# Values as a seven-product group: both groups opened on two token blocks, two convolution tiles moved into the heads

## The chip, the cores and the metric

The kernel runs on one core of a Trainium2 chip. The metric is device time in microseconds, from the median of several executions. One execution was profiled; its span runs from the first to the last instruction.

## The reference

One decoder layer over 512 tokens and 1024 channels, batch 1, all in float32. Cut to what matters here:

```python
u = _rmsnorm(h, norm1_g[l])
proj = u @ w_in[l]
a_glu, q, k, v, r, g_low, gate_a, gate_b = _split_cols(proj)
c = a_glu[..., :CONV_CH] * jax.nn.sigmoid(a_glu[..., CONV_CH:])
c = _causal_dwconv(c, conv_dw_w[l], conv_dw_b[l])            # width 31
c = jax.nn.silu(_layernorm(c, conv_ln_g[l], conv_ln_b[l]))
y_conv = c @ w_conv_out[l]
gk = jax.nn.log_sigmoid(g_low @ w_gate_up[l] + b_gate[l]) / GATE_NORMALIZER
o = _gla_chunked(qh, kh, vh, gkh)                            # 4 heads, chunks of 64
o = o * lax.rsqrt(jnp.mean(o * o, -1, keepdims=True) + EPS) * gla_norm_g[l]
o = o.reshape(bsz, seq, GLA_VDIM) * jax.nn.silu(r)
y_gla = o @ w_gla_out[l]
merged = jax.nn.sigmoid(gate_a) * y_conv + jax.nn.sigmoid(gate_b) * y_gla
h = h + merged @ w_o[l]
# then a channel mixer (up-projection, convolution of width 3, gate, down-projection) and a last RMSNorm
```

The change is in how `a_glu` (16 column tiles of 128), `v` and `r` (1024 columns each) are computed from `u`.

## The kernel before

**Arithmetic.** TensorE multiplies float32 operands rounded to a reduced format. Each operand is split into a high part (rounded by ACT) and a low part (the rest, subtracted by DVE), and `mm3` (lines 363 to 365) issues three matmuls: low by high, high by low, high by high. A weight block is 512 KB (128 partitions by 1024). `load` starts its transfer on SP's queue into one of four `raw` tiles, `split_weight` splits it into `whi` and `wlo` (four tiles each), and `weight` hands out the next block of one long list, `order`, having split those ahead of it. For blocks in `ADDED` the low part is not subtracted by DVE: ACT writes the negated raw block and POOL's queue adds the original onto its rounded form by an accumulating DMA.

**Tiles.** Convolution, query, key and gate projections are column tiles (`col_tile`): 128 output channels by 512 tokens, 24 matmuls for one weight block. Values and out-gate are laid out with tokens on partitions, because the heads read them so.

**Seven block products.** For names in `SEVEN` a product of two 2 by 2 block matrices is done with seven block products instead of eight (steps a11, a12, s1, n2, s4, n3, a22). The sums of activation blocks (`form`, `place`) are made by DVE, the sums of weight blocks by accumulating DMAs on POOL's queue (`sum_on`, `add_n3`) into the tile that `kept` names. Before, the out-gate `w_r` is such a group (`unit`), with blocks read from a relaid copy (`rows_r`) that 16 transfers from memory to memory on SP's queue (`lay_rows`) write early in the kernel.

**Order.** In the opening the order on PE, ACT, DVE and SP is written out by hand (`manual_schedule`): RMSNorm of four blocks of 128 tokens, their transposition, and the values' first 512 columns for all four token blocks (`v_block`, matmuls of line 624; the first two token blocks unnormalized, with the scale applied when the bank is read). Outside it a scheduler orders each engine. After the opening come the eight convolution tiles (gate and value block each), the low-rank decay projection, the out-gate's seven products with the gate arithmetic between them (`gate`, `GATE_AT`), then four heads. Between the heads' stages (`between`) stand matmuls that don't depend on them: the values' last 512 columns (`late_values`) and four gate tiles.

**Filling DVE.** The depthwise convolution is 30 DVE passes of 0.73 us per channel tile (line 740). These, the activation sums and the layer norm are `chains` of small jobs; every `weight` call lets `fill` emit as many as `RATES` says for that name, behind the latest instruction in `pace`.

Of the kernel before, what the change touches and what calls it, by code (L numbers as in the profile page):

```python
# [17 lines left out]
P = 128  # L18
# [19 lines left out]
RATES = {"w_glu": 6.2, "w_r": 0.3, "w_low": 0.0, "w_v": 5.0, "w_qk": 4.2, "w_gb": 6.0, "w_gla": 6.5, "w_ga": 9.0}  # L38
# [5 lines left out]
ADDED = {("w_glu", 2 * k) for k in range(1, KT)} | {(name, m) for name in ("w_gb", "w_gla") for m in range(KT)}  # L44
# [3 lines left out]
SEVEN = {"w_o": KT // 2, "w_down": FT // 2, "w_r": KT // 2}  # L48
# [5 lines left out]
R_STEPS = [("a11", 0), ("a11", 1), ("a12", 0), ("s1", 0), ("s1", 1), ("a12", 1)] + LATE  # L54
# [4 lines left out]
GATE_AT = [("a11", 1), ("a12", 0), ("n2", 1)]  # L59
# [16 lines left out]
def trunk_layer(ctx: ExitStack, tc: tile.TileContext, a: dict, out: bass.AP):  # L76
# [88 lines left out]
    order = [("w_v", j) for j in range(KT // 2)]  # L165
    order += [("w_glu", 2 * k + j) for k in range(KT) for j in (1, 0)]
    order += [("w_low", 0), ("w_low", 1)]
    order += [("w_r", (O_PAIRS, step, d)) for step, d in R_STEPS]
    for h in range(HEADS):
        late_v = [("w_v", KT // 2 + 2 * h + j) for j in range(2)]  # L170
        late_b = [("w_gb", 2 * (h - 2) + j) for j in range(2)]
        q, k = ("w_qk", 2 * h), ("w_qk", 2 * h + 1)
        order += [q, late_v[0], k, late_v[1]] if h == 0 else [q, k] + (late_v if h == 1 else late_b)
# [14 lines left out]
    def load():  # L188
        if len(raws) < len(order):
# [8 lines left out]
            if j is not None:  # L198
                raw = raw_tile()
                nc.sync.dma_start(raw, a[name][j])  # L200
# [17 lines left out]

    LOADS = {"a11": (0, 0), "a12": (1, 0), "n2": (1, 1), "n3": (0, 1)}

    def load_block(name, pairs, step, d):

        if step not in LOADS:
            return None
        src = block(name, pairs, d, *LOADS[step])
        n = src.shape[-1]
        if step == "a11":
            dst = keep_tile(name)[:, :n]
            kept[pairs, d] = dst
        else:  # L230
            dst = raw_tile()[:, :n]
        nc.sync.dma_start(dst, src)
        if step == "n3":
            kept[pairs, d, "n3"] = dst
            if name != "w_r":
                add_n3(name, pairs, d)
        if step == "n2":
            kept[pairs, d, "b22"] = dst
        return dst

    def add_n3(name, pairs, d):
        nc.gpsimd.dma_start(kept[pairs, d, "n3"], block(name, pairs, d, 1, 1), accum_op=ALU.add)

    def operand(name, raw, pairs, step, d):

        if step == "s4":
            return kept[pairs, d, "b22"]
        if step == "n2" and name != "w_r":
            nc.vector.tensor_tensor(kept[pairs, d], kept[pairs, d], raw, ALU.add)
        return raw if step in ("a12", "n3") else kept[pairs, d]  # L250
# [15 lines left out]
    def sum_on(name, pairs, step, d):  # L266

        where = {"a11": (0, 1), "n2": (1, 0)}
        if name == "w_r":
# [3 lines left out]
        if step in where:  # L273
            nxt = block(name, pairs, d, *where[step])
            nc.gpsimd.dma_start(kept[pairs, d], nxt, accum_op=ALU.add)

    def split_weight(between=None):
        if len(ready) < len(order):
# [34 lines left out]
            if order[len(ready)] in ADDED:  # L313
                nc.scalar.activation(lo, raw, AF.Copy, scale=-1.0)  # L314
# [15 lines left out]
    def weight(name, j, ahead=LOOK):  # L330
# [4 lines left out]
        fill(RATES.get(name, RATE))  # L335
# [4 lines left out]
    room = [0.0, 0]  # L340
    after = []

    def fill(n):
        room[0] += n
        while chains and room[0] > 0:
# [6 lines left out]
            if not chain:  # L352
                chains.remove(chain)
                if not chains and after:
# [147 lines left out]
    def turn_gain(i, bank):  # L502
        nc.tensor.transpose(bank[:, :KT], rows8[:KT, i * P : (i + 1) * P], ident[:KT, :KT])
        nc.vector.tensor_copy(gains[:, i * KT : (i + 1) * KT], bank[:, :KT])

    raise_clock(WARM)
    accs = [mm_bank() for _ in range(NT)]
    turn_gain(0, accs[2])
# [5 lines left out]
    def rms(t):  # L514
        ss = small(2, "ss")
        for j in range(2):
            nc.scalar.activation(junk(T), xs[t][j], AF.Square, scale=1.0 / 32.0, accum_out=ss[:, j : j + 1])
        v = small(1, "var")
        nc.vector.scalar_tensor_tensor(v, ss[:, 0:1], EPS, ss[:, 1:2], ALU.add, ALU.add)
        return rsqrt(v, 1)  # L520

    plain, r1 = {}, {}
# [55 lines left out]

    def renormed(t):
        rb = ax_bank()[:, :P]  # L580
        nc.tensor.matmul(rb, r1[t].to_broadcast([P, P]), ident, start=True, stop=True)
        rb = rb.unsqueeze(1).to_broadcast([P, 4, P])
        for g in range(2):
            nc.vector.tensor_tensor(into_whole(t, g)[0], by_token(unscaled[t, g]), rb, ALU.mult)
        for g in range(2):
            f, parts = into_whole(t, g)
            split_by(f, *parts)

    def gained_normed(t):
        for g in range(2):  # L590
            gain = gains[:, g * 4 : g * 4 + 4].unsqueeze(2).to_broadcast([P, 4, P])
            nc.vector.tensor_tensor(into_whole(t, g)[0], by_token(banks[t][g]), gain, ALU.mult)
        for g in range(2):
# [20 lines left out]
    def v_block(j, *ts, parts=None, more=False):  # L614
        for t in ts:
            src = as_landed(t) if t < 2 else tokens(t)
            ks = (2 * j, 2 * j + 1)
            todo = [(k, p) for p in parts for k in ks] if parts else [(k, p) for k in ks for p in ALL]
            for n, (k, p) in enumerate(todo):
                product(t, j, k, src, *p, j == 0 and n == 0 and not more, j == KT // 2 - 1 and n == len(todo) - 1)  # L620

    def product(t, j, k, src, a_low, w_low, first, last):
        w = ws[j][w_low][:, (k % 2) * T : (k % 2 + 1) * T]
        nc.tensor.matmul(accs[t], src(k)[a_low], w, start=first, stop=last)  # L624
# [1008 lines left out]
```

## Time and profile before

| | |
|---|---|
| median of three runs | 831.43 us (831.42 to 832.16) |
| the profiled execution's own time | 831.21 us |
| its span | 829.5 us, 10901 instructions |
| matmul records on PE | 4066 |
| mean granted TensorE clock | 0.997 |
| data moved | 127.21 MB, mean 153 GB/s |

PE is the matmul stream, PEld its weight loads, DVE, ACT and POOL the other engines, SP the engine that issues most transfers. A matmul's record spans its passage through the array and overlaps the next one's, so the distance of starts tells more than the duration. A row of a timeline or a chain gives start, duration and what ran; `x24` merges that many instructions; what stands in brackets is the idle time before it and what ended it.

### The profile page before, as it was taken

How to read it: one execution, taken by the hardware profiler on the slowest of the kernel's cores; microseconds unless marked ns; L12 is line 12 of the kernel's file. 1: busy time of each engine (PE TensorE's matmuls, PEld its weight loads, DVE VectorE, ACT ScalarE, POOL GpSimd, SP SyncE). 2: the span in 40 equal slices, each digit the busy share in tenths (PEclk: the TensorE clock that was granted, in tenths of full speed). 3: DMA queues.
4: the chain of work that ended last, by engine and by line, in shares of the span. 5: the costliest groups of instructions: out<-in, count | busy, mean ns of one | idle time of the engine just before them, and what ended most of it. 6: DMA issues, size and time to landing. Idle time of an engine off the chain costs nothing.

```text
span 829.5 us, 10901 instructions
## 1 busy us (share of the span) xinstructions
PE 818.6 (99%) x4066; PEld 692.3 (83%) x4066; DVE 667.5 (80%) x988; ACT 450.8 (54%) x648; POOL 106.2 (13%) x127
## 2 busy tenths in 40 slices
PE   9999999999999999999999999999999999999996
PEld 7888887888888888888888898888788888988885
DVE  6999966989899991875789788679858788588896
ACT  6843337762533553148544668655456543667554
POOL 2000102000111121000001012111112011220011
PEclk9999999999999999999999999999999999999998
DMA  9975547723546578221447639256825646657562
GB/s 340 303 205 143 137 110 170 210 101 101 128 110 153 133 195 199 102 82 54 143 97 189 189 119 262 68 145 153 216 87 148 171 87 219 153 153 196 136 126 102
DMA packets 43973, 127.21 MB, mean 153 GB/s; under 512 B 4272, under 2 KB 12736, under 8 KB 43920
## 3 DMA queue, kind: packets, MB, share of 16 engines
q1 hardware_dynamic: 33232, 88.82, 30.4%
q0 software_dynamic: 10512, 37.49, 25.5%
q8 instruction: 32, 0.52, 0.2%
q14 instruction: 21, 0.17, 0.1%
q10 hardware_dynamic: 176, 0.20, 0.1%
HBM read 124.40 MB, written 6.29 MB: 158 GB/s over the span
## 4 chain that ended last, share of the span: by engine, by line
PE 85%; DVE 5%; issue 4%; DMA 3%; ACT 2%; POOL 1%; POOLq 0%; SPq 0%; ACTq 0%; DVEq 0%
PE mm L363 24%; PE mm L364 24%; PE mm L365 24%; PE mm L624 3%; PE ax L363 2%; PE ax L364 2%; PE ax L365 2%; DMA kept<-in_w_o_dram 2%; DVE wlo L296 1%; PE ax L1051 1%; DMA raw<-in_w_o_dram 1%; DMA kept<-rows 1%; PE ax L1053 1%; PE ax L1033 1%; DVE tmp L1292 1%
## 5 line engine op out<-in xcount | busy, mean ns | idle before, releaser
L363 PE MATMUL mm<-uh,wlo 128*128 128x512 f32 (+1 forms) x620 | 234.7, 379 | 0.0
L364 PE MATMUL mm<-ul,whi 128*128 128x512 f32 (+1 forms) x620 | 232.3, 375 | 0.8 <-DVE ul L454 0.8
L365 PE MATMUL mm<-uh,whi 128*128 128x512 f32 (+1 forms) x620 | 231.8, 374 | 0.0
L740 DVE SCALAR_TENSOR_TENSOR c<-h,pp,c 128x507 f32<-128x507 f32 (+21 forms) x240 | 162.2, 731 | 1.2 <-ACT c L737 0.6
L365 PEld LDWEIGHTS mm<-uh,whi 128*128 128x128 f32 x620 | 116.7, 188 | 21.1
L364 PEld LDWEIGHTS mm<-ul,whi 128*128 128x128 f32 x620 | 116.9, 189 | 20.4 <-DVE ul L454 1.3
L363 PEld LDWEIGHTS mm<-uh,wlo 128*128 128x128 f32 x620 | 116.9, 189 | 19.0 <-issue 0.2
L312 ACT CAST whi<-raw 128x1024 fp32r<-128x1024 f32 x94 | 97.5, 1042 | 56.0 <-PE mm L365 43.3
L314 ACT ACTIVATE wlo<-raw 128x1024 fp32r<-128x1024 f32 x41 | 43.4, 1059 | 76.0 <-PE mm L363 68.8
L295 ACT CAST whi<-raw 128x1024 fp32r<-128x1024 f32 (+1 forms) x51 | 51.8, 1024 | 46.9 <-PE mm L365 35.0
L1292 DVE SCALAR_TENSOR_TENSOR tmp<-mm,pp,tmp 128x511 f32<-128x511 f32 x88 | 64.9, 744 | 10.6 <-ACT tmp L1290 10.1
L321 DVE TENSOR_TENSOR wlo<-raw,whi 128x1024 fp32r<-128x1024 f32 x53 | 64.3, 1220 | 10.4 <-ACT whi L312 9.7
L296 DVE TENSOR_TENSOR wlo<-raw,whi 128x1024 fp32r<-128x1024 f32 (+1 forms) x51 | 62.9, 1243 | 10.4 <-ACT whi L295 9.8
L295 ACT CAST whi<-kept 128x1024 fp32r<-128x1024 f32 (+1 forms) x40 | 40.0, 1006 | 33.8 <-PE mm L365 16.7
L296 DVE TENSOR_TENSOR wlo<-kept,whi 128x1024 fp32r<-128x1024 f32 (+1 forms) x40 | 46.6, 1168 | 14.4 <-ACT whi L295 14.2
L1290 ACT ACTIVATE tmp<-mm,pp 128x512 f32<-128x512 f32 x44 | 33.3, 774 | 12.0 <-PE mm L365 12.0
L1212 DVE TENSOR_TENSOR hres<-hres,mm 128x512 f32<-128x512 f32 (+1 forms) x49 | 32.5, 671 | 2.5 <-PE mm L365 2.3
L315 POOL DMA_DIRECT2D wlo<-in_w_up_dram x18 | 15.6, 864 | 98.0 <-ACT wlo L314 87.5
L364 PE MATMUL mm<-wlo,sh 128*128 128x512 f32 x66 | 25.9, 393 | 0.0
L365 PE MATMUL mm<-whi,sh 128*128 128x512 f32 x66 | 25.7, 390 | 0.0
L363 PE MATMUL mm<-whi,sl 128*128 128x512 f32 x66 | 25.2, 392 | 0.2 <-ACT whi L295 0.2
L364 PE MATMUL mm<-h,whi 128*128 128x512 f32 x64 | 25.0, 391 | 0.0
(360 smaller groups left out, 1629.4 us busy)
## 6 DMA issues: line engine op xcount, KB each, us to landing
raw<-in_w_up_dram SPq DMA_DIRECT2D x44, 512.0 KB, 4.9
wlo<-in_w_up_dram POOLq DMA_DIRECT2D x18, 512.0 KB, 7.7
raw<-in_w_glu_dram SPq DMA_DIRECT2D x16, 512.0 KB, 6.3
raw<-in_w_down_dram SPq DMA_DIRECT2D x15, 512.0 KB, 5.2
kept<-in_w_down_dram POOLq DMA_DIRECT2D x10, 512.0 KB, 5.3
raw<-in_w_v_dram SPq DMA_DIRECT2D x8, 512.0 KB, 5.5
rows<-in_w_r_dram SPq DMA_DIRECT2D x16, 256.0 KB, 6.7
raw<-in_w_qk_dram SPq DMA_DIRECT2D x8, 512.0 KB, 3.3
```

The source lines that it names most:

```text
L295: nc.scalar.copy(hi, raw)
L296: pace[0] = nc.vector.tensor_tensor(lo, raw, hi.bitcast(F32), ALU.subtract)
L312: nc.scalar.copy(hi, raw)
L314: nc.scalar.activation(lo, raw, AF.Copy, scale=-1.0)
L321: pace[0] = nc.vector.tensor_tensor(lo, raw, hi.bitcast(F32), ALU.subtract)
L363: nc.tensor.matmul(acc, ll, rh, start=first, stop=False, **kw)
L364: nc.tensor.matmul(acc, lh, rl, start=False, stop=False, **kw)
L365: nc.tensor.matmul(acc, lh, rh, start=False, stop=last, **kw)
L740: nc.vector.scalar_tensor_tensor(y[:, s:], c[:, : T - s], w, y[:, s:], ALU.mult, ALU.add)
L1212: nc.vector.tensor_tensor(hres[t, n][:, c], hres[t, n][:, c], x[:, c], op)
L1290: nc.scalar.activation(z, acc, AF.Identity, bias=pp[:, PP_FB + m : PP_FB + m + 1], scale=w[2])
L1292: nc.vector.scalar_tensor_tensor(z[:, s:], acc[:, : T - s], w[j], z[:, s:], ALU.mult, ALU.add)
```

## The change

The values become a group of seven block products like the out-gate, and both groups start in the opening. For the first two token blocks (256 tokens) the opening multiplies, for values and out-gate alike, the two block products a11 and a12, which need only the first 512 output columns: 16 matmuls of each of the three kinds per group. The sum of both is the finished quadrant; a11 alone is kept (`first_part`) and later written back to PSUM by ACT (`opened`), where the other products accumulate onto it. The remaining five products (s1, n2, s4, n3, a22) of the out-gate follow after five convolution tiles, those of the values after a sixth; the low-rank projection stands inside the values' group, and so do the gate steps. The inner dimension is paired as (0,4), (1,5), (2,6), (3,7). The last two convolution tiles take the place of the late values between the first heads' stages. The first convolution tile is multiplied in two halves of 256 tokens, the upper half of it in the opening. The out-gate's four opening blocks are read straight from its column layout by two transfers of 256 KB each. `RATES` are new, six query and key blocks join `ADDED`, one convolution block leaves it, and `ADDED` blocks now also set `pace`. The chain of the layer norm is started only when all eight convolution tiles have been begun.

```diff
-RATES = {"w_glu": 6.2, "w_r": 0.3, "w_low": 0.0, "w_v": 5.0, "w_qk": 4.2, "w_gb": 6.0, "w_gla": 6.5, "w_ga": 9.0}
+RATES = {"w_glu": 6.2, "late": 3, "w_r": 2, "w_low": 0.0, "w_v": 1, "w_qk": 4.5, "w_gb": 7, "w_gla": 10, "w_ga": 9.0}
-ADDED = {("w_glu", 2 * k) for k in range(1, KT)} | {(name, m) for name in ("w_gb", "w_gla") for m in range(KT)}
+ADDED = {("w_glu", 2 * k) for k in range(2, KT)} | {("w_qk", m) for m in range(2, KT)}
+ADDED |= {(name, m) for name in ("w_gb", "w_gla") for m in range(KT)}
-SEVEN = {"w_o": KT // 2, "w_down": FT // 2, "w_r": KT // 2}
+SEVEN = {"w_o": KT // 2, "w_down": FT // 2, "w_r": KT // 2, "w_v": KT // 2}
+IN_PAIRS = ((0, 4), (1, 5), (2, 6), (3, 7))
+IN_STEPS = [(step, d) for step in ("s1", "n2", "s4", "n3", "a22") for d in (0, 1)]
+GLU_AT = (5, 1, 2)
-GATE_AT = [("a11", 1), ("a12", 0), ("n2", 1)]
+GATE_AT = [("n2", 0), ("s4", 0), ("n3", 1)]
...
-    order = [("w_v", j) for j in range(KT // 2)]
-    order += [("w_glu", 2 * k + j) for k in range(KT) for j in (1, 0)]
-    order += [("w_low", 0), ("w_low", 1)]
-    order += [("w_r", (O_PAIRS, step, d)) for step, d in R_STEPS]
+    order = [("w_v0", j) for j in range(KT // 2)] + [("w_r0", j) for j in range(KT // 2)]
+    late = GLU_AT[0] + GLU_AT[1]
+    order += [("w_glu", 2 * k + j) for k in range(GLU_AT[0]) for j in (1, 0)]
+    order += [("w_r", (IN_PAIRS, step, d)) for step, d in IN_STEPS]
+    order += [("w_glu", 2 * k + j) for k in range(GLU_AT[0], late) for j in (1, 0)]
+    v_steps = [("w_v", (IN_PAIRS, step, d)) for step, d in IN_STEPS]
+    order += v_steps[:2] + [("w_low", 0), ("w_low", 1)] + v_steps[2:]
...
+            if name == "w_r0":
                 raw = raw_tile()
-                nc.sync.dma_start(raw, a[name][j])
+                for i in range(2):
+                    c = slice((2 * j + i) * P, (2 * j + i + 1) * P)
+                    dst = raw[:, i * T : (i + 1) * T].rearrange("p (c x) -> p c x", x=P)
+                    nc.sync.dma_start(dst, a["w_r"][:4, :, c].rearrange("c p x -> p c x"))
...
         nc.sync.dma_start(dst, src)
+        if step == "s1" and name in INNER:
+            nc.gpsimd.dma_start(dst, block(name, pairs, d, 0, 1), accum_op=ALU.add)
...
-                nc.scalar.activation(lo, raw, AF.Copy, scale=-1.0)
+                pace[0] = nc.scalar.activation(lo, raw, AF.Copy, scale=-1.0)
...
     block_ready()
-    v_block(2, 0, 1, parts=LOW_LAST)
-    r1[2] = rms(2)
+    v_block(2, 0, 1)
+    rms_squares(2)
+    rms(2)
     shrunk(2)
     banks[2] = turned(xs[2])
     block_ready()
-    r1[3] = rms(3)
+    v_block(3, 0, 1, parts=ALL)
+    rms_squares(3)
+    rms(3)
+    block_ready()
+    rms_squares(0)
     shrunk(3)
-    r1[0] = rms(0)
+    rms(0)
+    accs[2, 0], accs[2, 1] = mm_bank(), ax_bank()
+    v_block(4, 0)
     gained_normed(2)
-    v_block(3, 0, 1)
-    turn_gain(1, accs[3])
     banks[3] = turned(xs[3])
-    v_block(0, 2)
-    v_block(1, 2)
-    r1[1] = rms(1)
+    v_block(4, 1)
+    rms_squares(1)
+    block_ready()
+    rms(1)
+    split_normed(2)
+    v_block(5, 0, 1)
     gained_normed(3)
+    block_ready()
+    for t in range(2):
+        scaled_part("w_v", t, accs[0, t])
+    split_normed(3)
+    accs[3, 0], accs[3, 1] = mm_bank(), mm_bank()
+    v_block(6, 0, 1)
+    spreads = {t: spread_scale(t) for t in range(2)}
+    block_ready()
+    v_block(7, 0, 1)
+    gain_out(1, spread_bank[1][:, P:])
+    v_done(0)
+    wg = weight("w_glu", 1, 0)
+    pg = mm_bank()
+    col_tile(wg, acts1, pg, T // 2, T)
+    wa = weight("w_glu", 0, 0)
+    v_done(1)
     renormed(0)
...
+    pa = mm_bank()
+    col_tile(wa, acts1, pa, T // 2, T)
     renormed(1)
+    for t in range(2):
+        scaled_part("w_r", t, accs[2, t])
+    r_done(0)
+    r_done(1)
...
+    for k in range(GLU_AT[0]):
+        if k == 0:
+            col_tile(wg, acts1, pg, 0, T // 2)
+            col_tile(wa, acts1, pa, 0, T // 2)
+        for j in range(2 * k, min(2 * k + 2, KT)):
+            lay_rows(j)
+        glu_gate(k, None if k else pg)
+        glu_value(k, None if k else pa)
...
-    unit("w_r", quadrant, r_sink, r_at)
+    unit = Inner("w_r", sr)
+    unit.opened("x")
+    unit.run(IN_STEPS)
+    for k in range(GLU_AT[0], GLU_AT[0] + GLU_AT[1]):
+        glu_gate(k)
+        glu_value(k)
+    unit = Inner("w_v", vt)
+    unit.opened("x")
+    unit.run(IN_STEPS[:2])
+    glow = low_gate()
+    unit.run(IN_STEPS[2:], gate_at)
...
     def between(h, i):
         if h < 2:
-            late_values(2 * h + i)
+            (glu_value if h else glu_gate)(GLU_AT[0] + GLU_AT[1] + i)
         elif h < HEADS:
             gate_b(2 * (h - 2) + i)
```

The new class `Inner` that runs a group's five products; its `sink` copies or combines a finished bank into the result tiles:

```diff
+        def opened(self, which):
+            for i in range(2):
+                acc = self.bank[which, i] = ax_bank() if which == "z" else mm_bank()
+                nc.scalar.copy(acc, first_part[self.name, i])
...
+        def run(self, steps, at=lambda step, i: None):
+            steps = list(steps)
+            while steps:
+                step, d = steps.pop(0)
+                steps.pop(0)
+                parts = [(d, weight(self.name, (IN_PAIRS, step, d))) for d in (0, 1)]
+                for i in range(2):
+                    if step == "s1":
+                        self.bank["y", i] = mm_bank()
+                    acc = self.bank[self.OF[step], i]
+                    for d, w in parts:
+                        for j in range(2):
+                            ah, al = (x[:, i * P : (i + 1) * P] for x in quadrant(step, 2 * d + j))
+                            c = slice(j * T, (j + 1) * T)
+                            opens = step == "s1" and d == 0 and j == 0
+                            mm3(acc, (ah, al), (w[0][:, c], w[1][:, c]), opens, d == 1 and j == 1, step != "s1")
+                    self.sink(step, i, acc)
+                    at(step, i)
```

More of the change, by code (lines that the diff above doesn't have):

```diff
@@ L217, in keep_tile @@
         return fp.tile([P, D], F32, tag="kept", name=nm("kept"), bufs=2)
+    INNER = ("w_r", "w_v")
     LOADS = {"a11": (0, 0), "a12": (1, 0), "n2": (1, 1), "n3": (0, 1)}
     def load_block(name, pairs, step, d):
-        if step not in LOADS:
+        first = "s1" if name in INNER else "a11"
+        if step not in LOADS and step != first:
             return None
-        src = block(name, pairs, d, *LOADS[step])
+        src = block(name, pairs, d, *LOADS.get(step, (0, 0)))
         n = src.shape[-1]
-        if step == "a11":
+        if step == first:
             dst = keep_tile(name)[:, :n]
-            kept[pairs, d] = dst
+            kept[name, pairs, d] = dst
         else:
@@ L353, in fill @@
                 chains.remove(chain)
-                if not chains and after:
+                if not chains and after and begun[0] == KT:
                     chains.append(after.pop()())
@@ L702, in form @@
     def form(name, g):
-        q = lambda half, row: whole[half, g][:, row * T : (row + 1) * T]
+        q = lambda half, row: whole[half, row][:, g * T : (g + 1) * T]
         f = formed[name, g] = heap()
```

246 lines of the change are left out of this document (112 added, 134 removed).

## The prediction

> **What bounds the kernel.** I read the page's busy line first, then the chain that ended last, then the busy time by stage. All times are microseconds, from the start of the span of the profiled execution.
>
> ```profile
> PE 818.6 (99%) x4066; PEld 692.3 (83%) x4066; DVE 667.5 (80%) x988; ACT 450.8 (54%) x648; POOL 106.2 (13%) x127
> ...
> PE 85%; DVE 5%; issue 4%; DMA 3%; ACT 2%; POOL 1%; POOLq 0%; SPq 0%; ACTq 0%; DVEq 0%
> ```
>
> ```profile
> 0.00:33.00 33.00, 31.43 (x151) 26.02 (x152) 24.79 (x42) 23.79 (x47) 4.73 (x18) 1.00 0.96 329
> 33.00:100.00 67.00, 67.00 (x297) 55.49 (x296) 64.46 (x94) 33.12 (x42) 6.17 (x8) 1.00 0.66 179
> 100.00:150.00 50.00, 49.60 (x219) 40.71 (x218) 35.09 (x47) 28.75 (x39) 7.61 (x10) 1.00 0.65 147
> ...
> 200.00:310.00 110.00, 110.00 (x535) 92.59 (x534) 104.15 (x183) 52.00 (x90) 20.21 (x21) 1.00 0.56 140
> 310.00:350.00 40.00, 40.00 (x178) 33.14 (x177) 22.14 (x31) 10.21 (x10) 2.57 (x3) 1.00 0.59 145
> ```
>
> The columns after each stretch are its length and the busy time of PE, PEld, DVE, ACT and POOL, then clock, DMA share and GB/s. PE is never idle in the heads (200 to 310) and has 0.40 idle in 100 to 150, which holds the out-gate's products. So wherever this change removes products, PE is what the time waits for. Second is DVE: 64.46 of 67 in the convolution stage and 104.15 of 110 in the heads, yet PE did not wait there. The whole opening moves 329 GB/s at a DMA share of 0.96.
>
> A busy PE may hide slack, since one product's record overlaps the next. What a product costs is therefore read from the chain, where starts follow each other.
>
> ```profile
> 20.43 1.02 PE ax L442 x8
> ...
> 27.46 5.49 PE mm L624 x24
> ```
>
> ```profile
> 490.84 0.28 PE L365 MATMUL mm<-uh,whi 128*128 128x256 f32 x1
> ...
> 502.00 0.28 PE L365 MATMUL mm<-uh,whi 128*128 128x256 f32 x1
> ```
>
> 24 products of 512 columns took 5.49, so 0.229 each. Products of 256 columns started 93 times in 11.16, so 0.120 each.
>
> **Products removed.** One "product" below is one TensorE instruction; each multiplication of high and low parts issues three. Before: the opening 96 (four token blocks of the values' first half), the out-gate 7 block products of 24, 168, the late values 4 times 24, 96; together 360. After: the opening 96 (two token blocks, values and out-gate), and twice five block products of 24, 240; together 336. 24 fewer, and the chain has the price of exactly 24: **-5.49**. A single weight block now meets 12 products, 2.75, and a step of two blocks lasts 5.49.
>
> The Trainium skill, page "TensorE: Matmul & The Clock Gate", section "Back-to-back issue gap", gives about 131 ns for a sustained product of 512 columns; by it the saving would be 24 x 0.131 = 3.1. The 24 in the chain cost 229 ns each, so the measurement decides.
>
> **Half-width tile.** The first convolution tile's gate and value are multiplied in two halves, 96 products at 0.120 in place of 48 at 0.229: 11.52 - 10.98 = **+0.54**.
>
> **The opening.** It now needs eight weight blocks instead of four, and two more for the half tile inside it. The out-gate's blocks wait for the raw buffers as the convolution's blocks did before, so their landing is read from those.
>
> ```profile
> 7.42 3.69 SPq L102 DMA_DIRECT2D rows<-in_w_r_dram  x3
> 11.23 1.22 SPq L200 DMA_DIRECT2D raw<-in_w_glu_dram  x1
> ```
>
> ```profile
> raw<-in_w_glu_dram SPq DMA_DIRECT2D x1, 512.0 KB, 6.9
> ```
>
> ```profile
> 15.86 1.22 DVE L321 TENSOR_TENSOR wlo<-raw,whi 128x1024 fp32r<-128x1024 f32 x1
> ...
> 17.81 0.88 DVE L526 TENSOR_SCALAR h<-h,rstd 128x512 f32<-128x512 f32 x2 [0.67 <-POOL rstd L411]
> 18.61 0.15 DVE L519 SCALAR_TENSOR_TENSOR var<-ss 128x1 f32<-128x1 f32 x1
> 18.68 1.28 DVE L592 TENSOR_TENSOR f<-ax,gains 128x512 f32<-128x512 f32 x2
> 20.05 1.29 DVE L532 TENSOR_TENSOR ul<-f,uh 128x512 fp32r<-128x512 f32 x2
> ```
>
> ```profile
> L740 DVE SCALAR_TENSOR_TENSOR c<-h,pp,c 128x507 f32<-128x507 f32 (+21 forms) x240 | 162.2, 731 | 1.2 <-ACT c L737 0.6
> ...
> L295 ACT CAST whi<-kept 128x1024 fp32r<-128x1024 f32 (+1 forms) x40 | 40.0, 1006 | 33.8 <-PE mm L365 16.7
> ```
>
> The first out-gate block lands at 11.23 + 6.9 = 18.1; ACT's rounding (1.05 with the handover) is done at 19.2. DVE's order is written by hand, and from there up to the lower half of the first convolution tile it holds: six weight splits (four out-gate blocks, two convolution blocks) 7.32; shrinking 0.88; gain and split of token blocks 2 and 3, 2 x (1.28 + 1.29) = 5.14; the same two passes for blocks 0 and 1, 5.14; the values' two sums of parts, priced as a tap, 1.46; three small ones 0.45. That is 20.4 and ends at 39.6. PE gets there at 32.95 (the end of the old 96 products) plus 48 x 0.120 = 38.7. So PE waits 0.9: **+0.9**. It is 0 if the block lands a little sooner; the other end is a rival below. PE also turns block 3 into banks that block 2's gain pass must free first (20.43 in the chain); in the new order that pass ends at 19.2 + 1.22 + 0.88 + 0.15 + 1.28 = 22.7, and PE reaches the turning at 20.43 plus six products, 21.8. That wait is part of the same 0.9, since DVE's queue ends last.
>
> **Sums of weights.** Each block-product group adds weight blocks by POOL's accumulating DMAs: eight per group, as the out-gate had, now for two groups.
>
> ```profile
> kept<-rows POOLq DMA_DIRECT2D x3, 512.0 KB, 5.2
> ```
>
> ```profile
> 129.88 0.85 POOL L242 DMA_DIRECT2D raw<-rows  x1 [0.84 <-DMA raw<-rows]
> 130.89 0.89 POOL L275 DMA_DIRECT2D kept<-rows  x1 [0.16 <-issue]
> 141.31 0.86 POOL L242 DMA_DIRECT2D raw<-rows  x1 [9.54 <-DMA raw<-rows]
> 141.92 2.03 POOL L275 DMA_DIRECT2D kept<-rows  x2
> ```
>
> ```profile
> raw<-rows POOLq DMA_DIRECT2D x1, 512.0 KB, 5.9
> kept<-rows POOLq DMA_DIRECT2D x1, 512.0 KB, 9.2
> ```
>
> ```profile
> kept<-rows POOLq DMA_DIRECT2D x2, 512.0 KB, 8.4
> raw<-rows POOLq DMA_DIRECT2D x1, 512.0 KB, 5.2
> ```
>
> Alone one lands 5.2 after issue. Queued, 129.88 landed at 135.8 and 130.89 at 140.1, 4.3 apart; 141.31 landed at 146.5 and the pair behind it on average at 142.4 + 8.4 = 150.8, so 2.9 apart. Mean of the three: 3.4.
>
> Weight tiles have four buffers, so a block is split when the block four earlier is used up; the row of waits below (31 of ACT's roundings wait for PE) shows that it goes so.
>
> ```profile
> ACT whi L295 <- PE mm L365: 51.7, 31, 4.5
> ```
>
> Count from the first out-gate product after the opening, T. A split takes 1.05 + 1.22 = 2.3. In the out-gate's group the tightest sum is the second block of step n3. Three accumulates queue from T+2.4, when n2's second block is split; they land at 7.6, 11.0 and 14.4; the split is ready at 16.7 and is needed at 16.47 + 1.37 = 17.8. **0**, with 1.1 to spare. The next tight place is the convolution tile between the two groups, whose value block also goes through that queue. a22's first block is split at T+18.7, which frees the values' buffer; a load takes 3.5, and from 22.2 two accumulates for the values stand ahead of the tile's.
>
> ```profile
> raw<-rows SPq DMA_DIRECT2D x5, 512.0 KB, 3.5
> ...
> wlo<-in_w_glu_dram POOLq DMA_DIRECT2D x1, 512.0 KB, 7.9
> ```
>
> They land at 27.4, 30.8 and, the tile's, 34.2; PE needs it at 27.45 + 5.49 = 32.9. Late by 1.3, or not at all where POOL takes the tile's ahead of the second one (30.8). The order cannot be seen in this trace; I take the middle, **+0.7**. For the values' own group the two low-rank blocks stand between its first and second step and give it more room: 0.
>
> **What is hidden.** DVE gets six more splits (28 weight blocks instead of 22, 7.3) and six more combining passes (priced as taps, 4.4), and loses five splits that go to ACT and POOL (6.1): 5.6 more in all. In the out-gate's group two taps per block give 1.22 + 1.46 = 2.68 of 2.75, and four combining passes (2.9) put it some 2 behind over ten blocks, which the split-ahead of two blocks (5.5) covers. The two late convolution tiles cost PE nothing: they take the places of the late values, 24 products for 24. Six query and key splits leave the heads' DVE (7.3 of 104.15) for ACT (52.00 of 110). Ten taps per block in the next stage (7.3) exceed a block's 5.49, but in 310 to 350 DVE is busy only 22.14 of 40, since taps run ahead of their place; were that cover gone, each missing tap would hold the normalization by 0.73. Cost of all this: 0. The 0.40 idle of 100 to 150 goes with the old schedule: **-0.4**.
>
> **Sum.** -5.49 + 0.54 + 0.9 + 0.7 - 0.4 = -3.75. The profiled execution took 831.21 (span 829.5 and 1.7 around it), the median is 0.22 above it: 831.21 - 3.75 = 827.46, and 827.7 as a median.
>
> **Rivals.** (1) *The accumulating queue takes over* (slower). If each queued accumulate takes x instead of 3.4, the out-gate's n3 is late by 3x - 13.1 and the tile between the groups by 3x - 10.7. Without the queue term the sum is -4.45, so the change stops paying at 6x = 28.3, x = 4.7, and is slower by over 0.2% from x = 5.0. At 5.2, the time of one alone, it is 31.2 - 23.9 - 4.45 = +2.9: 834.3. For it: alone they take 5.2, and the convolution's accumulate above took 7.9. Against it: queued behind each other they came 4.3 and 2.9 apart. The Trainium skill, page "DMA: Bandwidth & Descriptors", section "Anatomy of one DMA — SWDGE (gpsimd) path", fits 2.0 plus bytes over 436e3, an estimate of 3.2 for 512 KB; by it neither place is late and the time is 827.0, but accumulates here took 5.2. Chance 0.17.
>
> (2) *The opening starves for weights* (no change).
>
> ```profile
> rows<-in_w_r_dram SPq DMA_DIRECT2D x16, 256.0 KB, 6.7
> ...
> x<-in_x_dram SPq DMA_DIRECT2D x3, 512.0 KB, 5.7
> ...
> pp<-in_pp_dram SPq DMA_DIRECT2D x1, 227.0 KB, 8.7
> ```
>
> Up to the half tile's value it needs 2.10 MB of x (three such blocks and two halves), ten blocks of 0.524, constants of 0.23, and the relay of the out-gate's weights, 16 x 0.262 = 4.19, if all of it goes first: 11.8 MB at 329 GB/s are 35.8. The gate block, one before the last, then lands at 34.2 and is split at 36.5, where PE wants it at 33.0: 3.5 in place of 0.9, a sum of -1.15, 830.3. For it: SP filled its idle time with relay transfers (7.42, three of them ahead of the first convolution block). Against: the hand-written order lets blocks go as soon as a buffer is free. Chance 0.14.
>
> (3) *Products give back less than their place in the chain.* Were the stream held by what every product shares, its weight load and issue, a removed product would give back only the pitch of the short ones, 1.02 / 8 = 0.128: 3.1 instead of 5.49, a sum of -1.3, 830.1. The short ones' own pitch and the gapless 0.229 of the long ones speak against it. Chance 0.03. The figure of the clock gate's page in the Trainium skill, above, would give the same time.
>
> (4) *No new wait at all*: -5.49 + 0.54 - 0.4 = -5.35, 826.1. Chance 0.04, beside 0.62 for the forecast.
>
> **Numbers.** 0.2% (1.66) is about what a measurement of this kernel tells from no change. Forecast and (4) are faster: 0.66; (2) and (3) within: 0.17; (1) slower: 0.17. The range goes from 0.3 below (4), for the spread of the runs, to 833.5, just short of (1) at 5.2: about 0.15 is left out.
>
> **What would show it.** Right: 24 products fewer before the heads; the first convolution tile starting near 33 and its lower half near 39.6 after a PE wait of about 1; PE idle under 1 in the out-gate's group; at most 1.3 ahead of the value tile between the groups. Wrong: PE waiting for a landing in the opening (rival 2); PE waits that end at an accumulate, more than 4.5 together (rival 1); a first convolution tile later than 35; or new PE waits in the heads, which I price at nothing.

## The result, and the profile after

The changed kernel takes 834.48 us (median of six runs, 833.06 to 835.67), the kernel before on the same chip 831.52 (830.57 to 832.33): a ratio of 1.0033, 95% interval 1.0020 to 1.0046. It is slower by 0.33%, where the prediction had 827.7 and a range up to 833.5. The profiled execution took 833.66, 2.45 more than the one before.

The page of the changed kernel first: the busy line, the chain's shares, and the costliest TensorE group, with its idle time and releaser at the end.

```profile
PE 816.5 (98%) x4090; PEld 691.1 (83%) x4090; DVE 676.4 (81%) x995; ACT 472.5 (57%) x672; POOL 117.7 (14%) x140
...
PE 72%; DVE 14%; DMA 6%; issue 4%; ACT 3%; POOL 1%; SPq 0%; POOLq 0%; ACTq 0%; DVEq 0%
...
L380 PE MATMUL mm<-uh,wlo 128*128 128x512 f32 (+1 forms) x636 | 238.1, 375 | 4.1 <-DMA wlo<-in_w_glu_dram 3.4
```

PE's busy time fell by 2.1 while the span grew by 2.4, and its share of the chain fell from 85% to 72%: PE now waits. The last row says where most of it is: 3.4 for one landing of a convolution tile's low part. The busy time by stage, same columns as before the change, places the rest.

```profile
0.00:33.00 33.00, 30.33 (x146) 24.33 (x147) 23.40 (x37) 22.66 (x43) 5.12 (x18) 1.00 1.00 328
33.00:100.00 67.00, 66.04 (x334) 56.17 (x334) 60.40 (x86) 35.69 (x47) 9.77 (x11) 1.00 0.84 219
100.00:150.00 50.00, 46.59 (x197) 37.73 (x196) 38.79 (x52) 25.45 (x33) 8.42 (x10) 0.97 0.82 194
...
200.00:310.00 110.00, 109.59 (x532) 92.24 (x530) 100.17 (x170) 53.47 (x90) 21.66 (x23) 1.00 0.65 152
```

PE's idle time went from 1.57 to 2.67 in the opening, from 0 to 0.96 in 33 to 100, from 0.40 to 3.41 in 100 to 150, and from 0 to 0.41 in the heads. The clock of 100 to 150 is 0.97 where it was 1.00.

**The wait between the groups.** The chain around it (start, length, what ran):

```profile
108.23 3.18 DMA kept<-in_w_v_dram
...
112.08 3.73 DMA kept<-in_w_v_dram
115.82 11.08 DMA wlo<-in_w_glu_dram
126.90 0.04 issue
126.94 0.50 PE mm L380
```

The accumulating transfer of the sixth convolution tile's value block was issued at 115.82 and landed at 126.90, 11.08 later. PE had nothing else from 123.37 on (its last product began at 123.14). The DMA issues of that stretch, from two short windows (KB, microseconds to landing):

```profile
kept<-in_w_v_dram POOLq DMA_DIRECT2D x1, 512.0 KB, 6.0
...
raw<-in_w_v_dram SPq DMA_DIRECT2D x2, 512.0 KB, 7.9
kept<-in_w_v_dram POOLq DMA_DIRECT2D x1, 512.0 KB, 8.9
```

Two accumulating transfers for the values' first sums stand ahead of it, issued at 112.08 and 115.18 and landed at 118.1 and 124.1. Beside them SP had two plain loads in flight, issued at 114.32 and 115.21. The trace has a landing for the second only, 7.9 after issue, where 3.5 was quoted before and the load just ahead of them (108.23 in the chain) took 3.18.

**A slower clock behind it.** TensorE alone around the wait: length, busy time with its count of products and the four other engines, then the granted clock.

```profile
123.00:127.00 4.00, 0.59 (x4) 0.17 (x2) 3.18 (x5) 2.82 (x5) 0.11 (x1) 1.00 1.06 215
127.00:130.50 3.50, 3.50 (x9) 2.79 (x10) 3.50 (x7) 0.69 (x1) 0.77 (x1) 0.55 1.08 217
130.50:135.00 4.50, 4.50 (x20) 3.65 (x20) 1.99 (x5) 0.66 (x1) 0.00 (x0) 0.97 0.58 165
```

Nine products ran in 3.5 after the wait, 20 in the next 4.5. From 126.94 to 131.16 there were 11 products in 4.22 where 11 x 0.229 = 2.52 would do: 1.7 more, on a stretch that the wait column calls busy.

**The opening.** Its chain, and PE at the first convolution tile's two halves:

```profile
27.84 6.06 DMA raw<-in_w_glu_dram
...
34.00 1.06 ACT whi L328
...
35.08 1.22 DVE wlo L337
...
41.57 0.39 PE mm L381
```

```profile
33.95 0.28 PE L380 MATMUL mm<-uh,wlo 128*128 128x256 f32 x1
...
40.85 0.50 PE L380 MATMUL mm<-uh,wlo 128*128 128x256 f32 x2 [0.70 <-ACT uh L553]
41.57 0.39 PE L381 MATMUL mm<-ul,whi 128*128 128x256 f32 x1 [0.22 <-DVE ul L554]
```

The upper half starts at 33.95, the lower one at 40.85 after a wait, with a second wait behind it. The chain leads back to the load of the tile's value block, issued on SP between relay transfers and landed at 33.90; DVE, whose order is written by hand, stood idle for it before 35.08, and everything behind that split came late.

**The balance.** For each product I took the distance to the next start and what it has over the usual 0.227 (512 columns) or 0.120 (256 columns), up to the heads' first attention product, which moved from 204.88 to 207.93, by +3.05:

| | before | after | difference |
|---|---|---|---|
| products of 512 / 256 columns | 836 / 6 | 764 / 102 | -4.82 |
| excess, 0 to 42 | 3.40 | 6.23 | +2.83 |
| excess, 42 to 115 | -0.11 | -0.08 | +0.03 |
| excess, 115 to 135 | 0.69 | 5.31 | +4.62 |
| excess, 135 to there | 0.60 | 0.92 | +0.32 |

The sum is +2.98. The 5.31 are the wait (3.57) and the slow stretch (1.7). Of the rest up to the end, 0.8 is a new wait in the heads (0.51 and 0.28 at line 1141, behind DVE's line 1135), and the untouched later stages came out shorter by 1.4, which I did not trace.

### The profile page after: what moved, and what is told of

It is laid out like the page before. It is cut to its first block, busy times and chain, and to the rows that moved or that the text cites. A ratio compares the mean times of both kernels' runs of the same rounds, so it can differ in the third digit from the quotient of the medians.

```text
span 831.9 us, 11028 instructions
## 1 busy us (share of the span) xinstructions
PE 816.5 (98%) x4090; PEld 691.1 (83%) x4090; DVE 676.4 (81%) x995; ACT 472.5 (57%) x672; POOL 117.7 (14%) x140
## 4 chain that ended last, share of the span: by engine, by line
PE 72%; DVE 14%; DMA 6%; issue 4%; ACT 3%; POOL 1%; SPq 0%; POOLq 0%; ACTq 0%; DVEq 0%
PE mm L381 21%; PE mm L382 21%; PE mm L380 21%; DVE c L797 4%; PE ax L380 2%; PE ax L381 2%; PE ax L382 2%; DVE wlo L312 2%; DVE wlo L337 1%; DMA wlo<-in_w_glu_dram 1%; ACT whi L311 1%; DMA raw<-in_w_down_dram 1%; DMA kept<-in_w_v_dram 1%; DVE hres L1283 1%; DVE tmp L1363 1%
## 5 line engine op out<-in xcount | busy, mean ns | idle before, releaser
L380 PE MATMUL mm<-uh,wlo 128*128 128x512 f32 (+1 forms) x636 | 238.1, 375 | 4.1 <-DMA wlo<-in_w_glu_dram 3.4
L797 DVE SCALAR_TENSOR_TENSOR c<-h,pp,c 128x507 f32<-128x507 f32 (+21 forms) x240 | 169.8, 731 | 2.8
L382 PEld LDWEIGHTS mm<-uh,whi 128*128 128x128 f32 x636 | 120.2, 189 | 20.6
L381 PEld LDWEIGHTS mm<-ul,whi 128*128 128x128 f32 x636 | 120.4, 189 | 19.3 <-DVE ul L471 0.6
L330 ACT ACTIVATE wlo<-raw 128x1024 fp32r<-128x1024 f32 x46 | 48.5, 1058 | 71.1 <-PE mm L380 69.4
L1363 DVE SCALAR_TENSOR_TENSOR tmp<-mm,pp,tmp 128x511 f32<-128x511 f32 (+1 forms) x88 | 64.6, 743 | 12.6 <-ACT tmp L1361 12.2
L337 DVE TENSOR_TENSOR wlo<-raw,whi 128x1024 fp32r<-128x1024 f32 x48 | 58.2, 1220 | 17.7 <-ACT whi L328 17.2
L311 ACT CAST whi<-kept 128x1024 fp32r<-128x1024 f32 (+1 forms) x44 | 44.2, 1009 | 42.3 <-PE mm L382 19.7
L312 DVE TENSOR_TENSOR wlo<-kept,whi 128x1024 fp32r<-128x1024 f32 (+1 forms) x44 | 51.4, 1172 | 11.2 <-ACT whi L311 11.0
L380 PE MATMUL mm<-h,wlo 128*128 128x512 f32 x64 | 25.4, 397 | 0.0
```

What stands on the lines that cost most here:

```text
L311: nc.scalar.copy(hi, raw)
L312: pace[0] = nc.vector.tensor_tensor(lo, raw, hi.bitcast(F32), ALU.subtract)
L330: pace[0] = nc.scalar.activation(lo, raw, AF.Copy, scale=-1.0)
L337: pace[0] = nc.vector.tensor_tensor(lo, raw, hi.bitcast(F32), ALU.subtract)
L380: nc.tensor.matmul(acc, ll, rh, start=first, stop=False, **kw)
L381: nc.tensor.matmul(acc, lh, rl, start=False, stop=False, **kw)
```

## The experiments

The theory behind the first six runs has two independent losses: POOL's accumulating queue between the groups (with the slow clock that its wait brings) and the landing of the tile's value block in the opening. The rivals were that DVE's order, or the place from which the convolution passes are let in (`pace`), makes the waits. The first four kernels to run were timed beside the kernel before at 832.13, the next three at 832.66 and the last three at 831.9; ratios are to those, and each section gives the difference of a ratio to the changed kernel's 1.0033 in microseconds.

**The tile's low part by DVE.** One block leaves `ADDED`.

```diff
-ADDED |= {(name, m) for name in ("w_gb", "w_gla") for m in range(KT)}
+ADDED |= {(name, m) for name in ("w_gb", "w_gla") for m in range(KT)}; ADDED -= {("w_glu", 10)}
```

> The value block of the sixth convolution tile (between the two groups) is split by DVE instead of by ACT and an accumulating DMA; nothing else is edited. Theory Q (the accumulating queue): in the changed kernel PE waits 3.57 us for this block's accumulate, third in POOL's queue (issued 115.82, landed 126.90), and then runs 3.5 us at a granted clock of 0.55, about 1.9 us lost. Both go: 5.5 us less than the changed kernel, about 829.0, and a clock of 1.00 in that stretch. Theory D (DVE and ACT are late there anyway, DVE is busy 3.00 of 3.00 us in 120 to 123): the wait only changes its releaser to DVE, 0 to 2 us less.

Measured 829.88, ratio 0.9972 (0.9962 to 0.9982), 0.61% under the changed kernel's ratio: 5.1. TensorE alone (length, busy time, clock):

```profile
123.00:127.00 4.00, 4.00 (x20) 1.00 0.95 224
```

The wait is gone, the clock stays at 1.00. One subtraction of 1.22 on DVE takes away both losses, so the slow stretch belongs to the wait. The same queue now holds PE for 1.2 at 155.6, in the values' own group.

**The relay behind the value block.** The 16 relay transfers are queued on SP behind the load of the first tile's value block.

```diff
-            nc.sync.dma_start(dst.rearrange("p (c x) -> p c x", x=P), src.rearrange("c p x -> p c x"))
+            with tc.issue_after(loads["w_glu", 0].ins): nc.sync.dma_start(dst.rearrange("p (c x) -> p c x", x=P), src.rearrange("c p x -> p c x"))
...
-                nc.sync.dma_start(raw, a[name.rstrip("0")][j])
+                loads[name, j] = nc.sync.dma_start(raw, a[name.rstrip("0")][j])
```

> The 16 relay transfers of the out-gate's weights are queued on SP behind the load of the first convolution tile's value block. Theory L (landing): in the opening DVE stands idle 1.92 us until that block, landed at 33.90, is rounded, and everything behind it in DVE's hand-written order is late; with the relay out of the way it lands by 31, the idle time goes, and the lower half of the first tile starts about 2 us earlier than 40.85: 1.5 to 2 us less, about 832.7. Theory W (DVE's own work of about 20 us sets the opening): 0.5 us less at most. Either way the out-gate's first kept blocks come later; if that bites, PE waits appear at the out-gate's s1 and the time grows.

Measured 831.81, ratio 0.9999 (0.9984 to 1.0014): 2.8 under the changed kernel. TensorE in the first tile, the changed kernel first, then this one with the place of the tile between the groups:

```profile
33.00:42.00 9.00, 8.04 (x58) 1.00 1.04 382
```

```profile
33.00:42.00 9.00, 9.00 (x77) 1.00 1.02 292
120.00:123.50 3.50, 0.52 (x3) 1.00 1.03 198
123.50:127.50 4.00, 3.60 (x10) 0.67 1.09 208
```

PE's idle time of 33 to 42 is gone: the first tile starts at 32.66 and its lower half at 38.41, in place of 33.95 and 40.85, and the out-gate's first product at 87.72 in place of 90.73. The other wait (3.53) and its slow stretch are still there, earlier by the gain. The two losses are independent.

**The values' first sums left out.** The two accumulating transfers ahead of the tile's are not issued.

```diff
-            nc.gpsimd.dma_start(dst, block(name, pairs, d, 0, 1), accum_op=ALU.add)
+            nc.gpsimd.dma_start(dst, block(name, pairs, d, 0, 1), accum_op=ALU.add) if name == "w_r" else None
```

> The accumulate that adds the second weight block to each of the values' two kept blocks at load is left out (the values' sums of blocks are then incomplete); the sixth tile's value block stays an accumulate. Theory Q: it is then alone in the queue, lands 6 us after its issue, about 122, before PE wants it at 123.1: wait and half clock go as in the run with the DVE split, 5.5 us less, about 829.0. Theory D: no accumulate in front changes nothing at ACT or DVE, the wait stays at 2 us or more.

Measured 829.48, ratio 0.9970 (0.9960 to 0.9979), as in the first experiment. The issues at the tile:

```profile
raw<-in_w_v_dram SPq DMA_DIRECT2D x1, 512.0 KB, 8.1
wlo<-in_w_glu_dram POOLq DMA_DIRECT2D x1, 512.0 KB, 7.9
```

PE does not wait. What stood ahead in the queue made the wait, not DVE. Yet alone in the queue the tile's transfer took 7.9, where the prediction had quoted 5.2 for one alone: a plain load beside it was in flight for 8.1.

**Pace from DVE.** The negation on ACT no longer sets `pace`.

```diff
-                pace[0] = nc.scalar.activation(lo, raw, AF.Copy, scale=-1.0)
+                nc.scalar.activation(lo, raw, AF.Copy, scale=-1.0)
```

> Blocks in ADDED no longer set pace, as before the change, so convolution taps stay queued behind the last split that DVE did. Theory P: the 0.8 us of PE wait at the first head's gated outputs (216.5, ended by DVE) comes from taps put ahead of the head's own DVE work; with the old pace it goes, 0.8 us less, about 833.7. Rival: the taps are as many as before and the old pace bunches them elsewhere, so the wait moves: no difference of more than 0.5 us.

Measured 836.97, ratio 1.0061 (1.0047 to 1.0075): 2.3 slower than the changed kernel, which neither theory had. The wait in the heads did vanish, but the one between the groups stayed (3.1, with 12 products at 0.43 behind it where the changed kernel had 7), and a new one of 2.7 came up much later, in the channel mixer, after the product that started at 516.90. That one is of use, TensorE alone again:

```profile
517.00:519.60 2.60, 0.29 (x2) 1.00 1.08 265
519.60:521.00 1.40, 1.18 (x5) 1.00 1.02 284
```

After this wait of 2.7 the clock is still 1.00; after the ones of 3.1 here and of 3.6 in the changed kernel it was not.

**The tile first in the queue.** The values' two sums are issued behind the tile's transfer.

```diff
-    pace = [None]
+    pace = [None]; held = []
...
-            nc.gpsimd.dma_start(dst, block(name, pairs, d, 0, 1), accum_op=ALU.add)
+            held.append((dst, block(name, pairs, d, 0, 1))) if name == "w_v" else nc.gpsimd.dma_start(dst, block(name, pairs, d, 0, 1), accum_op=ALU.add)
...
-                nc.gpsimd.dma_start(lo, a[name][spec], accum_op=ALU.add)
+                put = nc.gpsimd.dma_start(lo, a[name][spec], accum_op=ALU.add)
+                with tc.issue_after(put.ins): [nc.gpsimd.dma_start(*held.pop(0), accum_op=ALU.add) for _ in tuple(held)]
```

> The accumulating transfer of the sixth tile's value block is put ahead of the two for the values' first sums on POOL's queue; nothing else is changed against the changed kernel. Theory Q (the queue has too much to carry there, whatever its order): the tile's own wait goes, as it lands at about 122, and the two behind it land at about 128 and 133; with 2.3 for the split, the values' first block is ready at 130.3 and the second at 135.6, where PE wants them at 128.9 and 131.6, so a wait of 2.5 to 4 moves to the values' first products; if it comes in two pieces under 3 the clock stays at 1.00 and the time is 831 to 833. Rival O (only the order was wrong): no PE wait over 1 between 115 and 140, time 829 to 830, as where the tile left the queue.

Measured 842.33, ratio 1.0105 (1.0090 to 1.0121), worse than either theory had it. PE's waits from 115 to 170 (total, times, longest), and the issues:

```profile
PE mm L381 <- DVE wlo L312: 3.1, 2, 2.4
PE mm L380 <- ACT tmp L989: 2.3, 1, 2.3
PE mm L380 <- ACT whi L311: 2.2, 1, 2.2
PE mm L915 <- DVE h L816: 1.0, 1, 1.0
PE mm L380 <- DMA wlo<-in_w_glu_dram: 0.9, 1, 0.9
```

```profile
wlo<-in_w_glu_dram POOLq DMA_DIRECT2D x1, 512.0 KB, 8.8
...
kept<-in_w_v_dram POOLq DMA_DIRECT2D x2, 512.0 KB, 11.4
```

The wait moved to the values' products and grew, as the later sums of the group all came later too. The queue had too much to carry, and its order before was the better one. Its pieces were under 3, as the theory had it, and after two of 2.5 the clock stayed at 1.00; but behind a pair of 2.4 and 1.0 with one product between them (159.26 and 160.53) it fell all the same. The tile's own transfer, first in line beside plain loads, took 8.8 (issued 115.87, landed 124.70); the two behind it, with the plain loads done, landed at 127.0 and 129.5, only 2.3 and 2.6 apart.

**No loads beside.** That points to what makes the queue slow, so the two plain loads beside it were taken away.

```diff
-        nc.sync.dma_start(dst, src)
+        nc.vector.memset(dst, 0.0) if (name, step) == ("w_v", "n2") else nc.sync.dma_start(dst, src)
```

> The changed kernel without the two plain loads (1 MB) that run beside the three queued accumulating transfers ahead of the sixth convolution tile: the values' n2 blocks are set to zero by DVE instead (their part of the values is missing). Theory C (the accumulating transfers are slow because plain loads share the DMA engines with them): the first lands as before after about 6, the second 3 to 4.5 after it and the tile's 2.5 to 3.5 after that, at 121.5 to 124 in place of 126.9; the PE wait falls from 3.57 to 0 to 0.7 and the stretch of half clock goes, so 829 to 830. Rival N (the queue's own pace, 4.3 to 4.9 apiece, whatever runs beside): the tile's lands at 126 to 127, the wait stays over 3, the clock drops again, 834 to 835.

Measured 830.98, ratio 0.9988 (0.9979 to 0.9998), 3.7 under the changed kernel. The three transfers, issued at 113.07, 115.16 and 115.79, and TensorE at the tile (five engines):

```profile
kept<-in_w_v_dram POOLq DMA_DIRECT2D x1, 512.0 KB, 5.5
...
kept<-in_w_v_dram POOLq DMA_DIRECT2D x1, 512.0 KB, 5.9
wlo<-in_w_glu_dram POOLq DMA_DIRECT2D x1, 512.0 KB, 7.8
```

```profile
120.00:125.00 5.00, 5.00 (x23) 3.88 (x22) 5.00 (x8) 3.05 (x6) 1.39 (x2) 1.00 1.05 178
```

They landed at 118.6, 121.1 and 123.6, 2.5 apart, in place of 118.1, 124.1 and 126.9, which are 6.0 and 2.8 apart; PE does not wait and the clock holds. So the queue's own pace is 2.5 per transfer. The pitch of 6.0 is the one in which the plain loads moved, the last of them landing at 123.1. From the first issue to the last landing the three took 10.5 without the loads and 14.8 with them. The time is 1 above what was expected; the wait itself behaved as the theory of sharing said.

**Both undone.** The edits of the first two experiments together.

> The two edits of the earlier runs together: the value block of the sixth convolution tile has its low part subtracted by DVE again, and the relay of the out-gate's rows stands on SP's queue behind the load of the first convolution tile's value block. Theory A (the two waits are independent losses): each gives back what it gave alone, 4.6 to 5.1 and 2.7 to 2.8 against the changed kernel's 834.5, so 826.5 to 827.3, ratio to the kernel before about 0.994; no PE wait over 0.5 before 115 and no stretch with the clock under 0.9 after the opening. That is what 24 products fewer (-5.49), the half-width tile (+0.54) and the old idle (-0.4 to -0.6) make, with some 0.5 to 1 of small waits: it would confirm those terms of the sum. Rival B (removing one wait only uncovers another, so the gains do not add): 828.5 to 830, with a new PE wait of 1 to 3 in the values' group (130 to 160) or in the heads.

Measured 827.03, ratio 0.9936 (0.9916 to 0.9957), faster than before by 0.64% and 8.1 under the changed kernel's ratio, where the two alone gave 5.1 and 2.8: within the intervals they add up. But its profiled execution took 834.36, while the other eight took 825.2 to 827.8, and its chain says why:

```profile
143.01 12.12 DMA kept<-in_w_v_dram
```

```profile
155.00:159.70 4.70, 0.34 (x2) 0.84 0.04 15
159.70:165.00 5.30, 5.22 (x12) 0.50 0.01 3
```

The last sum of the values' group landed 12.12 after issue; ACT's rounding of it and the gate steps behind that on ACT ended at 159.7, PE waited 4.6, and the clock fell to half. So the values' group, to which the prediction gave room, is near the same edge. A further execution with its profile:

> The kernel with both waits undone once more, for one look, since its first profile holds a PE wait of 4.6 at 155 that its other executions by their times (825.2 to 827.8 against 834.4 for the profiled one) do not have. Expected: the values' accumulating transfers land in time, no PE wait over 1.3 between 120 and 165, clock 1.00 there, 826 to 828.

That execution took 832.55, with a wait of 2.5 at the same place: the expectation missed. TensorE alone, from there on:

```profile
155.00:160.00 5.00, 2.73 (x7) 0.76 0.02 5
160.00:165.00 5.00, 5.00 (x21) 0.90 0.28 103
```

Its clock fell to half as well: the starts around the wait are 2.77 apart, and of the products behind it seven came at 0.43. So a wait of 2.5 can bring the slow stretch, where one of 2.7 above did not.

The two kernels below, which have both edits as well, do not wait there in their profiled executions. In the two that do, the out-gate's accumulating transfers already landed late: the second of its four later sums at 91.8 and 92.6, against 89.6 and 87.7 in the two that don't. Why they did stays open.

**Fewer convolution passes beside the late tiles.** Both edits, and `"late": 1` in `RATES` in place of 3.

> As the run with both edits, and beside the two late convolution tiles only one convolution pass per weight block is put into DVE's order in place of three. Theory H (the PE wait of 0.5 and 0.3 for line 1135 in the heads comes from convolution passes standing ahead of it on DVE): that wait shrinks below 0.3 in sum and the time is 0.3 to 0.6 below the run with both edits, unless the passes that were held back are then missed in the next stage, where four passes left over would hold the normalization by 4 x 0.73 = 2.9. Rival: no difference over 0.3, the wait stays.

Measured 826.80, ratio 0.9926 (0.9913 to 0.9939), the same as with both edits within the intervals. The wait at line 1141 stayed (0.66 and 0.28). Ahead of it DVE's line 1135 itself stands idle 0.59 for POOL (line 428), so convolution passes in front of it are not the whole cause, and that theory of the heads is not borne out.

**Query and key splits back on DVE.** Both edits, and the six query and key blocks out of `ADDED`.

```diff
-ADDED = {("w_glu", 2 * k) for k in range(2, KT)} | {("w_qk", m) for m in range(2, KT)}
+ADDED = {("w_glu", 2 * k) for k in range(2, KT)}
```

> As the kernel with both waits undone, and the six query and key blocks have their low parts subtracted by DVE again as before the change: six splits of 1.22 (7.3) go back to DVE's heads, six negations (1.05) and six accumulating transfers go. By the prediction's step that hidden work costs nothing: 826.5 to 827.5, no PE wait over 0.5 for a weight in 165 to 310. Rival: DVE has no room in the heads now that two convolution tiles stand there, and PE waits 1 to 4 more there or in the layer norm, 828 to 831.

Measured 825.59, ratio 0.9931 (0.9912 to 0.9950). Busy time by stage:

```profile
33.00:100.00 67.00, 67.00 (x343) 57.43 (x342) 61.37 (x88) 36.74 (x49) 9.82 (x11) 1.00 0.95 240
100.00:150.00 50.00, 50.00 (x221) 41.08 (x220) 45.53 (x61) 30.64 (x40) 7.49 (x9) 1.00 0.85 214
...
200.00:310.00 110.00, 110.00 (x535) 92.87 (x535) 102.30 (x176) 52.96 (x90) 20.45 (x22) 1.00 0.61 143
```

PE is never idle from 33 to 310, with 102.30 on DVE in the heads. DVE had the room, so moving these six splits gained nothing, as the prediction's zero said. The last product ends at 817.31 where the kernel before had 822.87. With both edits the kernel beats the kernel before in all three forms that were timed; the three can't be told apart.

## Why the prediction was wrong

**Products and the half tile** (-5.49 + 0.54 = -4.95): -4.82 by counts and usual pitches. Right, and so is the price of 0.229 against the cheaper product of the third rival, under which the gain could be 3.0 at most (3.1 - 0.54 + 0.4). The kernels with both waits undone are 5.3 to 6.2 below the kernel before by their ratios, near the fourth rival's sum of -5.35, and the last of them is 5.1 ahead at the heads' first attention product (199.83 against 204.88).

**The queue** (+0.7): this is the step that failed. It had three queued transfers take 5.2, 3.4 and 3.4, the 3.4 as a mean of pitches in the old trace. So the tile's would land at T + 34.2, 1.3 after PE wants it at T + 32.9; as the order on the queue was unknown, about half of that was counted. With T at 90.7 much of this held: PE wanted the block at 123.4 (T + 32.9 is 123.6), and the first transfer landed at 118.1, which is T + 27.4, though by luck, issued 0.8 earlier than forecast and taking 6.0. The tile's was indeed the last of the three, which is 0.6 of the miss; it landed 2.0 later than T + 34.2, since the pitches were 6.0 and 2.8, and PE was 0.3 early. Together that takes the 0.7 to 3.57.

The old pitches were read as a property of the queue, when the plain loads beside it set them: 2.5 without, 6.0 with two of them. The old trace holds this, landing by landing. The pair priced there by its mean landed at 149.0 and 152.7. The pitch of 2.5 up to 149.0 has no plain load moving; those of 4.3 up to 140.1 and 3.7 up to 152.7 have one or more. That such loads would be there was to be had from the change itself, since the values' n2 blocks are loaded just there. The first rival is this mechanism and gave 3x - 10.7 = 4.1 for this place at the measured mean of 14.82 / 3 = 4.94 (measured 3.57); its other place, the out-gate's n3, was not late: those transfers were issued from 71.8 on and had landed by 83.5, ahead of T itself, so the race that was priced there did not take place.

The Trainium skill, page "DMA: Bandwidth & Descriptors", section "Queues, rings and completion order", says that each DMA engine goes round between the queues it has work for, a packet at a time. The trace agrees as to the sharing: between 118.1 and 124.1 the accumulating queue moved 0.68 MB and the plain one 0.80. No run here shows the turns themselves. Both sides pay: 7.9 for the second of two plain loads beside accumulating transfers, 4.5 for the second of two without any (issued at 398.4 in the changed kernel).

**The clock** was in no step: 1.7 more after the wait. The Trainium skill, page "TensorE: Matmul & The Clock Gate", section "What's actually happening", lets the clock fall to half after an idle window of about 3.4 us and rise after as long a busy one. The runs agree in part. Waits of 3.5, 3.6 and 4.6 brought half the clock, and two of 2.5 and one of 2.7 left it at 1.00; but one of 3.1 and another of 2.5, both shorter than that window, brought it too. Here the measurement decides: the length of a wait alone doesn't settle it between 2.5 and 2.7.

**The opening** (+0.9): 2.83, the second step that failed. The estimate followed DVE's hand-written order from 19.2 on, had DVE's own work end last, and assumed every weight block to be there in time. The order held, but DVE waited for the value block of the first tile, landed at 33.90 behind relay transfers. That is the second rival's mechanism, priced there at 3.5 for the gate block; the next block was the late one, and the relay was indeed ahead of it, as the second experiment shows. With the relay behind, the lower half starts at 38.41 without a wait, so DVE's own work, of which the 0.9 was made, cost nothing.

**Old idle** (-0.4): -0.7. **Heads and hidden work** (0): +0.8 in the profiled execution. This wait is absent where the query and key blocks do not set `pace` (pace from DVE, splits back on DVE), but also from both profiled executions of the kernel with both edits, where they do; its cause stays open. **Out-gate's group** (0): right in size, though not by the race that was priced.

Put together: -4.8 + 2.8 + 3.6 + 1.7 - 0.7 + 0.3 is the +3 measured up to the heads, within 0.1. Two terms of the sum were too small by 1.9 and 2.9, and one was missing, 1.7.

## What to carry to other kernels

A queue's pace that is read from an old trace holds only with the transfers that ran beside it: list what the change itself will load in the same stretch, and price the queue with that beside it. When a wait of 2.5 or more is in sight, price the slow stretch that can follow it as well, which no wait column shows. Where accumulating transfers bunch up, giving a single one back to an engine with room can be worth more than reordering the queue.

## What the runs showed of the hardware

Accumulating transfers of 512 KB that queue behind each other landed 2.3 to 2.8 apart when next to nothing else moved, and 6.0 apart while two plain loads did. The plain loads suffer too: the second of two took 7.9, against 4.5 without accumulating transfers and 3.2 alone.

A TensorE wait of 3.6 cost another 1.7, as seven products behind it came at 0.43 in place of 0.23. Behind waits of 2.5, 3.1, 3.5 and 4.6 in other runs, 7 to 12 products came at that pace. Two more of 2.5 and one of 2.7 cost only themselves.
